# A matmul-with-rope kernel in pairs of tiles, with half of the transposes done by VectorE in 32x32 blocks and loaded in column quarters

## The chip, the cores and the metric

One core of one Trainium2 chip. The metric is the device time of one execution in microseconds (us), the median of several runs; fast runs of one kernel agree within 1.5%. The rounds ran on different chips (numbers 0, 5, 6 and 12 are on record), so each has its own runs of the kernel before. Some executions are told "slow" (over 1.5% above the fastest of the same kernel); ratios and readings below use fast runs, unless a sentence says otherwise.

TensorE is the matmul engine (PE in the profile; PEld is its weight load), VectorE is DVE, ScalarE is ACT, GpSimd is POOL and SyncE is SP. SP issues nearly all loads and ACT nearly all stores, on two queues that the profile calls q1 (SP) and q10 (ACT). The profile counts both against the same 16 DMA engines.

## The reference

Input x is 16 x 512 x 768 in fp32, the weight is 768 x 768, cos and sin are 512 x 64.

```python
y = np.matmul(x, weight).reshape(batch, seq, n_heads, head_dim)   # 12 heads of 64
y1, y2 = y[..., :32], y[..., 32:]
out1 = y1 * cos1 - y2 * sin1
out2 = y2 * cos2 + y1 * sin2
out = np.concatenate([out1, out2], axis=-1).reshape(batch, seq, hidden)
```

## The kernel before

The 8192 rows are cut in 64 tiles of 128 rows. A tile goes through: load (SP), cast to fp16 (ACT), six 128x128 transposes (PE, into PSUM), a copy back to SBUF (ACT), twelve matmuls (PE, six chunks of the 768 columns times two parts of the output), two multiplies by cos and sin (DVE), an add (POOL) and a store (ACT's queue). Row p of tile r of a batch is sequence row 4p + r, so each partition gets a whole row of 3072 B.

```python
xv = x.rearrange("b (p r) h -> b r p h", r=SB)          # SB = 4

def load(i):
    xss[i] = xpool.tile([P, H], FP32, tag="xs", name="xs")
    nc.sync.dma_start(out=xss[i], in_=xv[i // SB, i % SB])

wv = weight.rearrange("(kt p) n -> p kt n", p=P)

def load_w(kt):
    nc.sync.dma_start(out=w_raw[:, kt], in_=wv[:, kt])  # 128 rows of 3072 B

def transpose(i, eng):
    ...
    for kt in range(NKT):                               # NKT = 6
        nc.tensor.transpose(pt[:, kt, :], xc[:, ts(kt, P)], ident)
    xTT[i] = tpool.tile([P, NKT, P], FP16, tag="xT", name="xT")
    copy(eng, xTT[i], pt)

def rope(i, c0, n, ps, add_eng):
    ...
    nc.vector.tensor_tensor(out=tv..., in0=ps..., in1=cos_sb[:, sb, :]..., op=MULT)
    nc.vector.tensor_tensor(out=qv..., in0=ps...[:, :, ::-1, :], in1=tee_sb[:, sb, :]..., op=MULT)
    add_eng.tensor_tensor(out=ov[:, ds(c0, n)], in0=tv, in1=qv, op=ADD)
```

## Time and profile before

The median is 166.50 us (166.46 to 166.57, 4 runs). The profiled execution is another that took 168.71 us; its span, from the first to the last instruction of the program, is 166.9 us.

| what | before | read from |
|---|---|---|
| PE busy | 153.6 of 166.9 us, 92% | the page's busy times |
| per tile on PE | 1.95 us matmuls + 0.34 us transposes | the timeline |
| per tile on DVE | 0.96 + 0.95 us | the groups by form |
| per tile on ACT, POOL | 0.84 + 0.80 us, 1.82 us | the groups |
| DMA packets of 3072, 1536, 1024 B | median 121, 65, 46 ns | the packets of the trace |

First the page of the kernel before: PE's busy time, then two rows with the span in 40 slices (DMA: mean busy share of the 16 engines in tenths, 9 is 90% or more; and what they moved), the SP queue (packets, MB, share of 16 engines), and the chain of waits by engine.

```profile
PE 153.6 (92%) x1165; PEld 98.5 (59%) x1165; DVE 122.9 (74%) x142; ACT 97.9 (59%) x127; POOL 114.4 (69%) x67
...
DMA  4999999999999999999999999999999984345544
GB/s 128 405 402 403 403 404 369 301 375 406 340 372 343 328 350 345 350 326 381 335 327 370 347 330 351 337 327 361 368 349 350 300 323 170 146 161 192 213 166 188
...
q1 hardware_dynamic: 10368, 27.92, 49.5%
...
PE 88%; DMA 4%; ACT 2%; DVE 2%; issue 1%; SPq 1%; DVEq 0%
```

PE is the limit: 92% busy and 88% of the chain that ended last. The DMA row is at 9 nearly throughout, which looks like a second limit, but it isn't one. The queue's own waits of SP (what, in all us, how often, longest) show what its loads waited for:

```profile
SPq L75 <- ACT xc L69: 83.2, 47, 1.9
```

47 loads waited, 83.2 us in all, for a cast to set an input buffer free. Loads run as far ahead as the buffers allow. A DMA share near 1 at 350 GB/s is therefore no proof that DMA bounds anything.

The costliest groups of the page (line, engine, operation, names, shapes, count | busy us, mean ns | idle before, and what ended it):

```profile
L130 POOL TENSOR_TENSOR ov<-tv,qv 128x768 f32<-128x768 f32 x63 | 114.2, 1816 | 47.4 <-DVE qv L122 46.2
L103 PE MATMUL psy<-w_sb,xT 128*128 128x512 f16 x756 | 135.1, 329 | 2.5 <-ACT xT L69 1.8
...
L116 DVE TENSOR_TENSOR tv<-psy,cos_sb 128x768 f32<-128x768 f32 (+1 forms) x65 | 61.4, 944 | 31.7 <-PE psy L103 30.5
L69 ACT COPY xT<-pt 128x768 f16<-128x768 f16 x63 | 50.3, 798 | 51.2 <-PE pt L93 51.2
L122 DVE TENSOR_TENSOR qv<-psy,tee_sb 128x768 f32<-128x768 f32 (+1 forms) x65 | 60.7, 934 | 0.0
L69 ACT CAST xc<-xs 128x768 f16<-128x768 f32 x63 | 52.7, 836 | 5.8 <-DMA xs<-in_x_dram 5.8
L93 PE MATMUL pt<-ident,xc 128*128 128x128 f16 x384 | 31.9, 219 | 2.9 <-ACT xc L69 2.2
```

Every other engine has less than PE's 2.285 us to do per tile: the largest is DVE, two multiplies.

### The profile page before, as it was taken

Reading aid. Unit: us, or ns where it says so; the run is one execution under the profiler, and the core shown is the slowest. Engines: PE = TensorE matmul, PEld = TensorE weight load, DVE = VectorE, ACT = ScalarE, POOL = GpSimd, SP = SyncE. Lnnn points to the kernel's source line nnn. Section 1 sums busy time; section 2 is a strip of 40 time slices with the busy share of each in tenths; the row PEclk is TensorE's granted clock in tenths of the full one; section 3 lists DMA queues with packets and bytes.
Section 4 is the critical chain, followed back from the end, with each engine's and each line's share of the span. In section 5 each row is a group of like instructions: output and inputs, shape, how many; then the busy total and the mean of one; then the engine's idle time right before and its main releaser. Section 6 shows DMA issues by size and latency. Waiting matters only on the chain.

```text
span 166.9 us, 3136 instructions
## 1 busy us (share of the span) xinstructions
PE 153.6 (92%) x1165; PEld 98.5 (59%) x1165; DVE 122.9 (74%) x142; ACT 97.9 (59%) x127; POOL 114.4 (69%) x67
## 2 busy tenths in 40 slices
PE   7657699999999999999999999999999999999930
PEld 2224466666666666666666666666666666666610
DVE  0522598777877688877778877778877778777792
ACT  3053366667766667766667766667666667666400
POOL 0000099777787777887777887777887777877770
PEclk9987999999999999999999999999999999999997
DMA  4999999999999999999999999999999984345544
GB/s 128 405 402 403 403 404 369 301 375 406 340 372 343 328 350 345 350 326 381 335 327 370 347 330 351 337 327 361 368 349 350 300 323 170 146 161 192 213 166 188
DMA packets 19887, 53.19 MB, mean 319 GB/s; under 512 B 2336, under 2 KB 2848, under 8 KB 19872
## 3 DMA queue, kind: packets, MB, share of 16 engines
q1 hardware_dynamic: 10368, 27.92, 49.5%
q10 hardware_dynamic: 9504, 25.07, 37.8%
q8 instruction: 9, 0.15, 0.5%
q14 instruction: 6, 0.05, 0.1%
HBM read 27.82 MB, written 25.17 MB: 317 GB/s over the span
## 4 chain that ended last, share of the span: by engine, by line
PE 88%; DMA 4%; ACT 2%; DVE 2%; issue 1%; SPq 1%; DVEq 0%
PE psy L103 74%; PE pt L93 13%; DMA xs<-in_x_dram 4%; PE psy L216 1%; DVE ov L130 1%; ACT xc L69 1%; ACT xT L69 1%; DVE qv L122 1%; SPq L80 1%; DVE tv L116 0%; SPq L75 0%; DVEq L130 0%; DVEq L116 0%
## 5 line engine op out<-in xcount | busy, mean ns | idle before, releaser
L130 POOL TENSOR_TENSOR ov<-tv,qv 128x768 f32<-128x768 f32 x63 | 114.2, 1816 | 47.4 <-DVE qv L122 46.2
L103 PE MATMUL psy<-w_sb,xT 128*128 128x512 f16 x756 | 135.1, 329 | 2.5 <-ACT xT L69 1.8
L103 PEld LDWEIGHTS <-xT 128*128 128x128 f16 x756 | 71.8, 99 | 44.9 <-ACT xT L69 2.1
L116 DVE TENSOR_TENSOR tv<-psy,cos_sb 128x768 f32<-128x768 f32 (+1 forms) x65 | 61.4, 944 | 31.7 <-PE psy L103 30.5
L69 ACT COPY xT<-pt 128x768 f16<-128x768 f16 x63 | 50.3, 798 | 51.2 <-PE pt L93 51.2
L122 DVE TENSOR_TENSOR qv<-psy,tee_sb 128x768 f32<-128x768 f32 (+1 forms) x65 | 60.7, 934 | 0.0
L69 ACT CAST xc<-xs 128x768 f16<-128x768 f32 x63 | 52.7, 836 | 5.8 <-DMA xs<-in_x_dram 5.8
L93 PE MATMUL pt<-ident,xc 128*128 128x128 f16 x384 | 31.9, 219 | 2.9 <-ACT xc L69 2.2
L93 PEld LDWEIGHTS <-xc 128*128 128x128 f16 x384 | 26.6, 98 | 12.3 <-ACT xc L69 3.0
L83 DVE CAST w_sb<-w_raw 128x768 f16<-128x768 f32 x6 | 3.3, 558 | 4.1 <-DMA w_raw<-in_weight_dram 4.1
L141 PE MATMUL cold_ps<-cold 128*128 128x512 f16 x13 | 4.6, 514 | 1.2 <-DVE cold L146 1.2
L141 PEld LDWEIGHTS <-cold 128*128 128x128 f16 x13 | 1.5, 126 | 3.3 <-issue 1.9
L71 DVE CAST xc<-xs 128x768 f16<-128x768 f32 x1 | 0.6, 560 | 3.7 <-DMA xs<-in_x_dram 3.7
L69 ACT ACT_TABLE_LOAD x1 | 1.3, 1283 | 2.1 <-issue 2.1
L216 PE MATMUL psy<-w_sb,xT 128*128 128x384 f16 x12 | 2.1, 326 | 0.0
L130 DVE TENSOR_TENSOR ov<-tv,qv 128x384 f32<-128x384 f32 x2 | 1.7, 862 | 0.1
L216 PEld LDWEIGHTS <-xT 128*128 128x128 f16 x12 | 1.2, 98 | 0.8
L71 DVE COPY xT<-pt 128x768 f16<-128x768 f16 x1 | 0.6, 556 | 0.6 <-PE pt L93 0.6
L146 DVE MEMSET cold<- 128x256 uint32 x1 | 0.3, 272 | 0.9 <-PEq L244 0.9
L244 POOL MEMSET const-float32-0.0<- 128x1 f32 x1 | 0.1, 98 | 0.2 <-issue 0.2
L185 DVE TENSOR_SCALAR tee_sb<-tee_sb 128x128 f32<-128x128 f32 x1 | 0.2, 220 | 0.0
L244 POOL MEMSET const-bfloat16-1.0<- 128x1 bf16 x1 | 0.1, 101 | 0.0
(2 smaller groups left out, 0.2 us busy)
## 6 DMA issues: line engine op xcount, KB each, us to landing
xs<-in_x_dram SPq DMA_DIRECT2D x64, 384.0 KB, 5.6
out_dram<-ov ACTq DMA_DIRECT2D x63, 384.0 KB, 4.8
w_raw<-in_weight_dram SPq DMA_DIRECT2D x6, 384.0 KB, 5.9
out_dram<-ov SPq DMA_DIRECT2D x2, 192.0 KB, 2.2
cos_sb<-in_cos_dram ACTq DMA_DIRECT2D x1, 128.0 KB, 5.2
tee_sb<-in_sin_dram ACTq DMA_DIRECT2D x1, 128.0 KB, 6.2
ident<-identity ACTq DMA_DIRECT2D x1, 32.0 KB, 3.6
```

Source lines behind the costliest of these rows:

```text
L69: eng.copy(out=o, in_=i_)
L71: eng.tensor_copy(out=o, in_=i_)
L80: nc.sync.dma_start(out=w_raw[:, kt], in_=wv[:, kt])
L83: nc.vector.tensor_copy(out=w_sb[:, kt], in_=w_raw[:, kt])
L93: nc.tensor.transpose(pt[:, kt, :], xc[:, ts(kt, P)], ident)
L103: nc.tensor.matmul(psys[i][:, ds(noff, nsz)], xTT[i][:, kt, :], w_sb[:, kt, ds(noff % H, nsz)], start=(kt == 0), stop=(kt == NKT - 1),)
L116: nc.vector.tensor_tensor(out=tv.rearrange("p (h d) -> p h d", d=D), in0=ps.rearrange("p (h d) -> p h d", d=D), in1=cos_sb[:, sb, :].unsqu ...
L122: nc.vector.tensor_tensor(out=qv.rearrange("p (h t d) -> p h t d", t=2, d=HD), in0=ps.rearrange("p (h t d) -> p h t d", t=2, d=HD)[:, :, : ...
L130: add_eng.tensor_tensor(out=ov[:, ds(c0, n)], in0=tv, in1=qv, op=ADD)
L141: nc.tensor.matmul(cold_ps, cold[:, 0:P], cold, start=True, stop=True)
L146: nc.vector.memset(cold, 0.0)
L216: nc.tensor.matmul(psys[i][:, n, 0:sz], xTT[i][:, kt, :], w_sb[:, kt, ds(c0, sz)], start=(kt == 0), stop=(kt == NKT - 1),)
```

## The change

The intent is to give PE and DVE less to do.

1. Tiles are worked in pairs from two batches with the same rows, so the same cos and sin. One multiply of 3072 elements per partition (cos and sin products of both tiles) takes the place of four of 768.
2. The second tile of each pair isn't transposed by PE. DVE transposes it, and the kernel takes it that DVE's transpose works on 32x32 blocks, each by itself. So a block stays within its group of 32 partitions, and a group can hold only one quarter of the columns. The load has to put it there: group q of 32 partitions gets the column quarter q (192 columns, 768 B) of all 128 rows.
3. The weight rows have to follow the same order of columns: partition 32q + a of chunk (t, e) holds row 192q + 64t + 2a + e.

```diff
-    def load(i):
-        xss[i] = xpool.tile([P, H], FP32, tag="xs", name="xs")
-        nc.sync.dma_start(out=xss[i], in_=xv[i // SB, i % SB])
+    def load(n, s):
+        b, r = where(n, s)                      # 2 * (n // SB) + s, n % SB
+        ...
+        if by_blocks(n, s):                     # n > 1 and s == 1
+            xs = xs.rearrange("p (j k) -> p j k", j=NQ)
+            src = x[b].rearrange("(j a r) (q k) -> r j q a k", r=SB, a=R, q=NQ)
+            for j in range(NQ):
+                nc.sync.dma_start(out=xs[:, j], in_=src[r, j])
+        else:
+            nc.sync.dma_start(out=xs, in_=x[b].rearrange("(p r) h -> r p h", r=SB)[r])
-    wv = weight.rearrange("(kt p) n -> p kt n", p=P)
-        nc.sync.dma_start(out=w_raw[:, kt], in_=wv[:, kt])
+    wv = weight.rearrange("(q t a e) n -> t e q a n", q=NQ, t=NT, e=2)
+        nc.sync.dma_start(out=w_raw[:, t, e], in_=wv[t, e])
+    def transpose_blocks(n, s):
+        xT = tpool.tile([P, NT, P, 2], FP16, tag="xT", name="xT")
+        nc.vector.transpose(
+            out=xT.bitcast(FP32).rearrange("p t m e -> p (t m e)"),
+            in_=x16.pop((n, s)).bitcast(FP32).rearrange("p t j r -> p (t j r)"),
+        )
+        xTT[n, s] = xT.rearrange("p t m e -> p t e m")      # PE reads every second element
     def rope(...):
-        (two multiplies of 768)
+        nc.vector.tensor_tensor(                             # one of 3072
+            out=tq..., in0=psys[n]...broadcast_to((P, 2, nh, D)),
+            in1=csn[:, :, r, :]...broadcast_to((P, 2, nh, D)), op=MULT)
...
```

The change also has a longer prefetch (8 pairs instead of 8 tiles), other buffer counts and another order of start and end, which the cut above leaves out.

More of the change, by code (lines that the diff above doesn't have):

```diff
@@ L34, with where, by_blocks @@
     HD = D // 2
-    NKT = H // P
-    NMB = B * S // P
+    R = 32
+    NQ = P // R
+    KQ = H // NQ
+    NT = KQ // (2 * R)
     SB = S // P
-    NSPLIT = [(0, 512), (512, H - 512)]
-    HALVES = [(0, H // 2), (H // 2, H // 2)]
-    FIRST = 3
-    AHEAD = 8
-    xv = x.rearrange("b (p r) h -> b r p h", r=SB)
-    ov_dram = out.rearrange("b (p r) h -> b r p h", r=SB)
+    NP = B * SB // 2
+    CHUNKS = [(t, e) for t in range(NT) for e in range(2)]
+    DEPTH = 8
+    TAIL = 2
+    def where(n, s):
+        return 2 * (n // SB) + s, n % SB
+    def by_blocks(n, s):
+        return n > 1 and s == 1
     konst = ctx.enter_context(tc.tile_pool(name="konst", bufs=1))
     ident = konst.tile([P, P], FP16)
-    cos_sb = konst.tile([P, SB, D], FP32)
-    tee_sb = konst.tile([P, SB, D], FP32)
-    w_raw = konst.tile([P, NKT, H], FP32)
-    w_sb = konst.tile([P, NKT, H], FP16)
-    xpool = ctx.enter_context(tc.tile_pool(name="xpool", bufs=AHEAD + 3))
-    cpool = ctx.enter_context(tc.tile_pool(name="cpool", bufs=4))
-    tpool = ctx.enter_context(tc.tile_pool(name="tpool", bufs=FIRST + 2))
-    rpool = ctx.enter_context(tc.tile_pool(name="rpool", bufs=4))
-    opool = ctx.enter_context(tc.tile_pool(name="opool", bufs=5))
+    cold = konst.tile([P, 512], FP16)
+    sin_sb = konst.tile([P, SB, D], FP32)
+    csn = konst.tile([P, 2, SB, D], FP32)
+    w_raw = konst.tile([P, NT, 2, H], FP32)
+    w_sb = konst.tile([P, NT, 2, H], FP16)
+    xpool = ctx.enter_context(tc.tile_pool(name="xpool", bufs=2 * DEPTH + 2))
+    cpool = ctx.enter_context(tc.tile_pool(name="cpool", bufs=6))
+    tpool = ctx.enter_context(tc.tile_pool(name="tpool", bufs=7))
+    rpool = ctx.enter_context(tc.tile_pool(name="rpool", bufs=3))
+    opool = ctx.enter_context(tc.tile_pool(name="opool", bufs=4))
     pt_pool = ctx.enter_context(tc.tile_pool(name="pt", bufs=2, space=bass.MemoryType.PSUM))
-    py_pool = ctx.enter_context(tc.tile_pool(name="py", bufs=3, space=bass.MemoryType.PSUM))
-    cold = konst.tile([P, 512], FP16)
+    py_pool = ctx.enter_context(tc.tile_pool(name="py", bufs=2, space=bass.MemoryType.PSUM))
     cold_ps = pt_pool.tile([P, 512], FP32, tag="pt", name="cold_ps")
-    xss, x16, xTT, psys, ovs = {}, {}, {}, {}, {}
+    xss, x16, xTT, psys, tqs, ovs = {}, {}, {}, {}, {}, {}
     def copy(eng, o, i_):
@@ L71, in copy @@
             eng.tensor_copy(out=o, in_=i_)
-    def load(i):
-        xss[i] = xpool.tile([P, H], FP32, tag="xs", name="xs")
-        nc.sync.dma_start(out=xss[i], in_=xv[i // SB, i % SB])
-    wv = weight.rearrange("(kt p) n -> p kt n", p=P)
-    def load_w(kt):
-        nc.sync.dma_start(out=w_raw[:, kt], in_=wv[:, kt])
-    def cast_w(kt):
-        nc.vector.tensor_copy(out=w_sb[:, kt], in_=w_raw[:, kt])
-    def cast(i, eng):
-        x16[i] = cpool.tile([P, H], FP16, tag="xc", name="xc")
-        copy(eng, x16[i], xss.pop(i))
@@ L89, in transpose @@
-    def transpose(i, eng):
-        xc = x16.pop(i)
-        pt = pt_pool.tile([P, NKT, P], FP16, tag="pt", name="pt")
-        for kt in range(NKT):
-            nc.tensor.transpose(pt[:, kt, :], xc[:, ts(kt, P)], ident)
-        xTT[i] = tpool.tile([P, NKT, P], FP16, tag="xT", name="xT")
-        copy(eng, xTT[i], pt)
-    def mm(i, kt, parts=NSPLIT):
-        if i not in psys:
-            psys[i] = py_pool.tile([P, 2, 512], FP32, tag="psy", name="psy").rearrange(
+    def load(n, s):
+        b, r = where(n, s)
+        xs = xpool.tile([P, H], FP32, tag="xs", name="xs")
+        if by_blocks(n, s):
[4 more added lines that the diff above has]
+        else:
+            nc.sync.dma_start(
+                out=xs, in_=x[b].rearrange("(p r) h -> r p h", r=SB)[r]
+            )
+        xss[n, s] = xs
@@ new lines, with load_w, cast_w, cast @@
+    wv = weight.rearrange("(q t a e) n -> t e q a n", q=NQ, t=NT, e=2)
+    def load_w(t, e):
+        nc.sync.dma_start(out=w_raw[:, t, e], in_=wv[t, e])
+    def cast_w(t, e):
+        nc.vector.tensor_copy(out=w_sb[:, t, e], in_=w_raw[:, t, e])
+    def cast(n, s, eng):
+        xc = cpool.tile([P, H], FP16, tag="xc", name="xc")
+        x16[n, s] = xc.rearrange("p (t q r) -> p t q r", t=NT, q=NQ)
+        src = xss.pop((n, s))
+        if by_blocks(n, s):
+            src = src.rearrange("p j (t r) -> p t j r", t=NT)
+        else:
+            src = src.rearrange("p (q t r) -> p t q r", t=NT, q=NQ)
+        copy(eng, x16[n, s], src)
@@ new lines, in transpose @@
+    def transpose(n, s, eng):
+        xc = x16.pop((n, s)).rearrange("p t q (r e) -> p t e (q r)", e=2)
+        pt = pt_pool.tile([P, NT, 2, P], FP16, tag="pt", name="pt")
+        for t, e in CHUNKS:
+            nc.tensor.transpose(pt[:, t, e, :], xc[:, t, e, :], ident)
+        xT = tpool.tile([P, NT, 2, P], FP16, tag="xT", name="xT")
+        copy(eng, xT, pt)
+        xTT[n, s] = xT
+    def transpose_blocks(n, s):
[3 more added lines that the diff above has]
+            in_=x16.pop((n, s)).bitcast(FP32).rearrange("p t j r -> p (t j r)"),
+        )
+        xTT[n, s] = xT.rearrange("p t m e -> p t e m")
@@ L100, in mm @@
+    def mm(n, s, t, e, c0=0, c1=H):
+        if n not in psys:
+            psys[n] = py_pool.tile([P, 3, 512], FP32, tag="psy", name="psy").rearrange(
                 "p b n -> p (b n)"
             )
-        for noff, nsz in parts:
-            nc.tensor.matmul(
-                psys[i][:, ds(noff, nsz)],
-                xTT[i][:, kt, :],
-                w_sb[:, kt, ds(noff % H, nsz)],
-                start=(kt == 0),
-                stop=(kt == NKT - 1),
-            )
-    def rope(i, c0, n, ps, add_eng):
-        sb = i % SB
-        nh = n // D
-        tv = rpool.tile([P, H], FP32, tag="tv", name="tv")[:, :n]
-        qv = rpool.tile([P, H], FP32, tag="qv", name="qv")[:, :n]
+            if n < 2:
+                nc.tensor.matmul(
+                    psys[n][:, 512:1024], cold[:, 0:P], cold, start=True, stop=False
+                )
+        cut = 512 if s == 0 else 256
+        for lo, hi in ((0, cut), (cut, H)):
+            lo, hi = max(lo, c0), min(hi, c1)
+            joined = n < 2 and 512 <= s * H + lo < 1024
+            if lo < hi:
+                nc.tensor.matmul(
+                    psys[n][:, ds(s * H + lo, hi - lo)],
+                    xTT[n, s][:, t, e, :],
+                    w_sb[:, t, e, ds(lo, hi - lo)],
+                    start=((t, e) == CHUNKS[0] and not joined),
+                    stop=((t, e) == CHUNKS[-1] and not (joined and s == 0)),
+                )
@@ L116, in rope @@
+    def rope(n, c0, c1, add_eng):
+        r = n % SB
+        w = c1 - c0
+        nh = w // D
+        if n not in tqs:
+            tqs[n] = rpool.tile([P, 2, 2 * H], FP32, tag="tq", name="tq")
+            ovs[n] = opool.tile([P, 2 * H], FP32, tag="ov", name="ov")
+        tq = tqs[n][:, :, ds(c0, w)]
+        ov = ovs[n][:, ds(c0, w)]
         nc.vector.tensor_tensor(
-            out=tv.rearrange("p (h d) -> p h d", d=D),
-            in0=ps.rearrange("p (h d) -> p h d", d=D),
-            in1=cos_sb[:, sb, :].unsqueeze(1).broadcast_to((P, nh, D)),
+            out=tq.rearrange("p j (h d) -> p j h d", d=D),
+            in0=psys[n][:, ds(c0, w)].rearrange("p (h d) -> p h d", d=D)
+            .unsqueeze(1).broadcast_to((P, 2, nh, D)),
+            in1=csn[:, :, r, :].unsqueeze(2).broadcast_to((P, 2, nh, D)),
@@ L120, in rope @@
             op=MULT,
         )
-        nc.vector.tensor_tensor(
-            out=qv.rearrange("p (h t d) -> p h t d", t=2, d=HD),
-            in0=ps.rearrange("p (h t d) -> p h t d", t=2, d=HD)[:, :, ::-1, :],
-            in1=tee_sb[:, sb, :].rearrange("p (t d) -> p t d", t=2)
-            .unsqueeze(1).broadcast_to((P, nh, 2, HD)),
-            op=MULT,
-        )
-        ov = ovs[i]
-        add_eng.tensor_tensor(out=ov[:, ds(c0, n)], in0=tv, in1=qv, op=ADD)
-    def rope_whole(i):
-        ovs[i] = opool.tile([P, H], FP32, tag="ov", name="ov")
-        rope(i, 0, H, psys.pop(i)[:, 0:H], nc.gpsimd)
@@ L136, in store @@
-    def store(i):
-        nc.scalar.dma_start(out=ov_dram[i // SB, i % SB], in_=ovs.pop(i))
-    def warm(n):
-        for _ in range(n):
+        add_eng.tensor_tensor(
+            out=ov.rearrange("p (h t d) -> p h t d", t=2, d=HD),
+            in0=tq[:, 0].rearrange("p (h t d) -> p h t d", t=2, d=HD),
+            in1=tq[:, 1].rearrange("p (h t d) -> p h t d", t=2, d=HD)[:, :, ::-1, :],
+            op=ADD,
+        )
+    def store(n, eng, c0=0, c1=2 * H):
+        b, r = where(n, 0)
+        dst = out.rearrange("b (p r) h -> r p b h", r=SB)[r, :, b : b + 2]
+        src = ovs[n].rearrange("p (b h) -> p b h", b=2)
+        if c1 - c0 < 2 * H:
+            s = c0 // H
+            dst = dst[:, s, c0 - s * H : c1 - s * H]
+            src = src[:, s, c0 - s * H : c1 - s * H]
+        eng.dma_start(out=dst, in_=src)
@@ L141, in warm @@
+    def warm(k):
+        for _ in range(k):
             nc.tensor.matmul(cold_ps, cold[:, 0:P], cold, start=True, stop=True)
@@ L147 @@
     nc.scalar.dma_start(out=ident, in_=id_dram.ap())
-    load(0)
-    load_w(0)
-    load_w(1)
-    load(1)
-    nc.scalar.dma_start(out=cos_sb, in_=cos.rearrange("(p r) d -> p r d", r=SB))
-    nc.scalar.dma_start(out=tee_sb, in_=sin.rearrange("(p r) d -> p r d", r=SB))
-    load_w(2)
-    load_w(3)
-    load(2)
-    load_w(4)
-    load_w(5)
-    for i in range(FIRST, AHEAD):
-        load(i)
-    warm(9)
-    cast(0, nc.vector)
-    transpose(0, nc.vector)
-    warm(4)
-    for kt in (0, 1):
-        cast_w(kt)
-        mm(0, kt)
@@ L169 @@
-    cast(1, nc.scalar)
-    transpose(1, nc.scalar)
-    mm(1, 0)
-    mm(1, 1)
-    for kt in (2, 3):
-        cast_w(kt)
-        mm(0, kt)
-        mm(1, kt)
-    cast(2, nc.scalar)
-    transpose(2, nc.scalar)
-    for kt in range(4):
-        mm(2, kt)
-    cast_w(4)
-    for i in range(FIRST):
-        mm(i, 4)
-    cast_w(5)
+    for n in (0, 1):
+        for s in (0, 1):
+            load(n, s)
+    for t, e in CHUNKS:
+        load_w(t, e)
+    load(2, 0)
+    nc.sync.dma_start(out=csn[:, 0], in_=cos.rearrange("(p r) d -> p r d", r=SB))
@@ new lines @@
+    nc.sync.dma_start(out=sin_sb, in_=sin.rearrange("(p r) d -> p r d", r=SB))
+    load(2, 1)
+    for n in range(3, DEPTH):
+        for s in (0, 1):
+            load(n, s)
+    warm(8)
+    cast(0, 0, nc.vector)
+    transpose(0, 0, nc.vector)
+    cast(0, 1, nc.scalar)
+    warm(4)
+    transpose(0, 1, nc.scalar)
+    cast(1, 0, nc.vector)
+    warm(4)
+    transpose(1, 0, nc.vector)
+    cast(1, 1, nc.scalar)
+    warm(4)
+    transpose(1, 1, nc.scalar)
+    for k, c in enumerate(CHUNKS):
+        cast_w(*c)
+        mm(0, 0, *c)
+        mm(0, 1, *c)
+        if k == 0:
+            continue
+        mm(1, 0, *CHUNKS[k - 1])
@@ L185 @@
+    cast(2, 0, nc.scalar)
+    cast(2, 1, nc.scalar)
+    nc.vector.tensor_copy(out=csn[:, 1, :, 0:HD], in_=sin_sb[:, :, HD:D])
     nc.vector.tensor_scalar_mul(
-        out=tee_sb[:, :, 0:HD], in0=tee_sb[:, :, 0:HD], scalar1=-1.0
+        out=csn[:, 1, :, HD:D], in0=sin_sb[:, :, 0:HD], scalar1=-1.0
     )
-    cast(3, nc.scalar)
-    mm(0, 5)
-    rope_whole(0)
-    mm(1, 5)
-    rope_whole(1)
-    transpose(3, nc.scalar)
-    cast(4, nc.scalar)
-    mm(2, 5)
-    rope_whole(2)
-    for i in range(FIRST, NMB):
-        if i + AHEAD - FIRST < NMB:
-            load(i + AHEAD - FIRST)
-        if i + 1 < NMB:
-            transpose(i + 1, nc.scalar)
-        if 4 < i + 2 < NMB:
-            cast(i + 2, nc.scalar)
-        if i < NMB - 1:
-            for kt in range(NKT):
-                mm(i, kt)
-            rope_whole(i)
-            store(i - 3)
@@ L210 @@
-    i = NMB - 1
-    ovs[i] = opool.tile([P, H], FP32, tag="ov", name="ov")
-    for n, (c0, sz) in enumerate(HALVES):
-        for kt in range(NKT):
-            if i not in psys:
-                psys[i] = py_pool.tile([P, 2, 512], FP32, tag="psy", name="psy")
-            nc.tensor.matmul(
-                psys[i][:, n, 0:sz],
-                xTT[i][:, kt, :],
-                w_sb[:, kt, ds(c0, sz)],
-                start=(kt == 0),
-                stop=(kt == NKT - 1),
-            )
-    for j in range(NMB - 4, NMB - 1):
-        store(j)
@@ L225 @@
-    for n, (c0, sz) in enumerate(HALVES):
-        rope(i, c0, sz, psys[i][:, n, 0:sz], nc.vector)
-        nc.sync.dma_start(out=ov_dram[i // SB, i % SB, :, ds(c0, sz)], in_=ovs[i][:, ds(c0, sz)])
+    rope(0, 0, 2 * H, nc.gpsimd)
+    mm(1, 0, *CHUNKS[-1])
+    transpose(2, 0, nc.scalar)
+    for c in CHUNKS:
+        mm(1, 1, *c)
+    transpose_blocks(2, 1)
+    cast(3, 0, nc.scalar)
+    cast(3, 1, nc.scalar)
+    rope(1, 0, 2 * H, nc.gpsimd)
+    transpose_blocks(3, 1)
+    for n in range(2, NP):
+        if n + DEPTH - 2 < NP:
+            for s in (0, 1):
+                load(n + DEPTH - 2, s)
+        if n < NP - 1:
+            for c in CHUNKS:
+                mm(n, 0, *c)
+            if n + 1 < NP:
+                transpose(n + 1, 0, nc.scalar)
+            for c in CHUNKS:
+                mm(n, 1, *c)
+            if n + 2 < NP:
+                cast(n + 2, 0, nc.scalar)
+                cast(n + 2, 1, nc.scalar)
+            if n >= 3:
+                store(n - 3, nc.scalar)
+            if n < NP - TAIL:
+                rope(n, 0, 2 * H, nc.gpsimd)
+            else:
+                rope(n, 0, H, nc.gpsimd)
+                rope(n, H, 2 * H, nc.gpsimd)
+            if n + 2 < NP:
+                transpose_blocks(n + 2, 1)
@@ L231 @@
+    n = NP - 1
+    for c in CHUNKS:
+        mm(n, 0, *c)
+    for c in CHUNKS:
+        mm(n, 1, *c, 0, H // 3)
+    for c in CHUNKS:
+        mm(n, 1, *c, H // 3, H)
+    store(n - 3, nc.scalar)
+    store(n - 2, nc.scalar)
+    store(n - 1, nc.sync)
+    rope(n, 0, H, nc.gpsimd)
+    store(n, nc.scalar, 0, H)
+    m = H + H // 3
+    rope(n, H, m, nc.gpsimd)
+    rope(n, m, 2 * H, nc.vector)
+    store(n, nc.sync, H, m)
+    store(n, nc.scalar, m, 2 * H)
 _INS = ['x', 'weight', 'cos', 'sin', 'n_heads']
```

## The prediction

> **What bounds it now.** TensorE: on the page PE is busy 92% of 166.9 us, and the chain of waits is 88% PE. From 21 us to 160 us it repeats, per 128-row tile, 1.95 us of matmuls plus 0.34 us for six transposes: 2.285 us x 61 = 139 us; the tail is 6 us. The groups give, per tile, VectorE 0.96 + 0.95 us, ScalarE 0.84 + 0.80, GpSimd 1.82, all below that. Most DMA packets of 3072 B take 121 ns, of 1536 B about 65, of 1024 B 46: about 8 ns + 0.037 ns per byte on one DMA engine. Loads run about 11 tiles ahead; nothing in the steady state waits for them.
>
> **Engines after the change, per pair of tiles (estimates from those durations).** PE: 2 x 1.95 + 0.34 = 4.24 us instead of 4.57. VectorE: one 3072-element multiply, from 957 ns at 768 and 550 at 384 about 3.4 us instead of 3.8, plus a transpose of about 0.55: 3.95. GpSimd about 3.6, ScalarE 2.5. Two pairs fit in PSUM, so it stays PE-bound: 30 x 4.24 plus a shorter start would give about 151 us, if loads kept up. Strided weight loads (step 2) should cost nothing visible.
>
> **What decides it: the loads.** The quarter loads and all six weight loads now walk DRAM as 4 column quarters x 32 rows, the 4 outermost; the tile side is 128 partitions. [...] Before, transfers had 128 outermost: 16 engines[...]. After, it gives 4[...]. Their work, estimated with the packet times above:
> - weights 6 x 32 x 121 ns = 23 us (6 us over 16 engines);
> - quarter loads 30 tiles x 4 x 32 packets of 768 B at about 37 ns = 141 us;
> - whole loads 34 x 8 x 121 ns = 33 us, stores 64 x 8 x 121 ns = 62 us.
> Together 259 us that the other twelve engines can't relieve; per pair 4.7 + 0.97 + 1.94 = 7.6 us against 4.24 of PE. So the span becomes DMA-bound: 2 us to the first packet, 259, less the last five pairs' stores (10), plus about 11 after the last load: about 264 us, with rounding and latency.
>
> **Predicted: 264 us, 230 to 288. Faster by over 2%: 0.20; within 2%: 0.02; slower by over 2%: 0.78.** The faster share is the case that transfers spread over 16 engines after all (about 151 us).
>
> **What would show it.** The DMA row's mean busy share falls from 0.98 to 0.4 to 0.6, GB/s to about 200. A weight load takes about 4 us by itself; the last weight chunk's matmuls start near 31 us instead of 14. Casts on ScalarE wait for loads in every pair; the chain of waits is mostly DMA; PE busy falls near 60%, and its granted clock may drop in the gaps. Multiply 3.4 us, block transpose 0.55, GpSimd add 3.6 test the engine costs.
>
> **What would make it wrong.** A spread over 16 engines (then 151 us, unless the GpSimd add with reversed halves takes over 4.24 us and bounds it); 768 B packets far from 37 ns; four engines running faster while twelve idle.

The sum: 23 + 141 + 33 + 62 = 259 us, and 2 + 259 - 10 + 11 = 262, "about 264" with rounding and latency. But the four engines that the first two terms are divided by, and that all four terms fall on the same ones, were the estimate when this was written. The trace of the kernel after shows the four (1112 end packets, below); that they are the same ones is inferred there. Two pairs do fit in PSUM: the kernel after ran with two such buffers.

## The result

The kernel after takes 268.92 us (median of 267.36 to 270.26, 4 fast runs), beside 166.50 us before: ratio 1.6147, 95% interval 1.6055 to 1.624, slower. A ratio is the mean time of one kernel's fast runs over that of the other's fast runs of the same rounds, so it isn't quite the ratio of the medians quoted. The predicted 264 us is 1.8% below the median.

The page of the kernel after, the same rows and the granted TensorE clock (in tenths) besides:

```profile
PE 168.5 (63%) x994; PEld 95.0 (36%) x994; DVE 131.6 (49%) x79; ACT 73.3 (27%) x95; POOL 110.0 (41%) x38
...
PEclk9955569998898997997557797989996599999995
DMA  6225255466665657564546646666554678646386
GB/s 237 104 103 161 100 150 166 136 232 227 229 216 197 220 175 246 187 228 149 165 136 231 224 163 209 227 218 211 202 199 138 228 264 332 257 163 236 146 328 236
...
q1 hardware_dynamic: 22232, 28.71, 32.8%
...
SPq 39%; DMA 35%; POOL 10%; issue 8%; ACT 2%; PE 2%; DVE 1%; POOLq 0%; ACTq 0%; DVEq 0%
```

PE fell from 92% to 63% busy and DMA from about 320 to 199 GB/s in the mean, with a share of 0.5 to 0.6. In the second and third slice (7 to 20 us), when the weights are loaded, the share is 2 tenths and the rate 103 to 104 GB/s: a quarter of the 402 to 405 GB/s that the kernel before reached in its second to sixth slice. SyncE's queue heads the chain, at 39%. I read that as back-pressure and not as a longer instruction: issuing a whole-tile load, a plain transfer like the one before, took SP 1.56 us in the median instead of 0.33.

Two of the waits (who waited for what: us in all, times, longest us) of the kernel after:

```profile
ACT xT L76 <- DMA xs<-in_x_dram: 71.8, 9, 21.9
...
ACT xc L76 <- DMA xs<-in_x_dram: 52.7, 13, 21.3
```

ScalarE waits for loads, singly up to 22 us. (The first line is no cast: the copy xT needs no load, but stands behind a store in ACT's order, which waits for a load to land; see cols4 below.) In the kernel before, the casts' wait for loads came to 5.8 us, all at the start. The longest piece of the chain, in order of time (start us, us, what), is the weights:

```profile
8.55 23.09 DMA w_raw<-in_weight_dram
```

And the group of the weight casts (engine, operation, times of one, first and last start), with what it waited for:

```profile
L100 DVE CAST w_sb<-w_raw x6: 559/560/561, 11.6 to 31.7; 128x768 f16<-128x768 f32 x6
...
  DMA w_raw<-in_weight_dram: 19.0, 6
```

Six casts from 11.6 to 31.7 us, on average 4.0 us apart. Last, the engine costs, from the groups by form:

```profile
L169 POOL TENSOR_TENSOR ov<-tq 128x1536 f32<-128x1536 f32 x30 | 103.4, 3449 | 152.7 <-DMA out_dram<-ov 107.1 <-DVE tq L162 45.6
L162 DVE TENSOR_TENSOR tq<-psy,csn 128x3072 f32<-128x3072 f32 x30 | 100.5, 3351 | 43.2 <-PE psy L145 43.1
L145 PEld LDWEIGHTS <-xT 128*128 128x128 f16 x768 | 78.0, 105 | 150.7 <-ACT xT L76 83.5 <-issue 28.3
...
L123 DVE STREAM_TRANSPOSE xT<-xc 128x384 f32<-128x384 f32 x30 | 17.2, 575 | 60.0 <-ACT xc L76 60.0
```

The packets of the trace tell how many engines took part, by their number. Before, the SP queue had 72 transfers and 1152 packets of 4 bytes, 16 for each. I read them as one end packet from each engine that works on a transfer. After:

| SP transfers of the kernel after | count | engines if all 16 | engines if quarters and weights use 4 |
|---|---|---|---|
| whole tiles of x | 34 | 544 | 544 |
| column quarters | 120 | 1920 | 480 |
| weights | 6 | 96 | 24 |
| cos, sin, last stores | 4 | 64 | 64 |
| sum (measured: 1112) | 164 | 2624 | 1112 |

The count is 1112 exactly: quarter loads and weights, with four entries in the slowest dimension in DRAM, ran on four engines. Which four they are, the packets don't tell; that they are always the same four is inferred from the rate of 103 to 104 GB/s above, with several weight loads in flight: from 9 to 20 us four packets are under way in 88% of the moments (sampled every 10 ns), five or six in the rest, never fewer. The time follows from the packet times, summed: quarter packets 567 us over 4 engines = 142 us, weights 768 packets at about 0.13 us over 4 = 25 us, the other loads about 43 us over 16, and the stores 62 us over 16. That is 272 us of packet time on each of the four engines, more than the span of 266.7 us: packets of one engine then overlap in time (the share of all 16, a sum of packet times too, came to 1.03 from 8 to 25 us in the kernel before), so the sum tells that the four were full, and isn't itself a time. (The third term is the rest of the loads' packet time after the weights.) In every stretch that I summed between 10 and 220 us (20 to 40 us each), it comes to 1.10 to 1.16 of the stretch. The other twelve engines have 105 us of packet time.

The loads don't bind to the end, though. The last packet of 768 B ends at 234.1 us, and from 217 us on PE runs without a stop, a pair every 4.24 us. The last issue of quarter loads and the last matmuls of the timeline:

```profile
215.15 8.09 SPq L87 DMA_DIRECT2D xs<-in_x_dram  x4
...
251.62 6.01 PE L145 MATMUL psy<-w_sb,xT 128*128 128x256 f16 x36
```

### The profile page after: what moved, and what is told of

Its sections match the earlier page's. It is cut to its first block, busy times and chain, and to the rows that moved or that the text cites. A ratio compares the mean times of both kernels' runs of the same rounds, so it can differ in the third digit from the quotient of the medians.

```text
span 266.7 us, 2682 instructions
## 1 busy us (share of the span) xinstructions
PE 168.5 (63%) x994; PEld 95.0 (36%) x994; DVE 131.6 (49%) x79; ACT 73.3 (27%) x95; POOL 110.0 (41%) x38
## 4 chain that ended last, share of the span: by engine, by line
SPq 39%; DMA 35%; POOL 10%; issue 8%; ACT 2%; PE 2%; DVE 1%; POOLq 0%; ACTq 0%; DVEq 0%
SPq L87 26%; DMA xs<-in_x_dram 18%; SPq L89 11%; POOL ov L169 10%; DMA w_raw<-in_weight_dram 9%; DMA out_dram<-ov 8%; PE psy L145 2%; SPq L97 2%; ACT xc L76 2%; DVE tq L162 1%; ACT xT L76 1%; POOLq L315 0%; ACTq L184 0%; PE pt L116 0%; ACTq L76 0%
## 5 line engine op out<-in xcount | busy, mean ns | idle before, releaser
L145 PE MATMUL psy<-w_sb,xT 128*128 128x512 f16 (+1 forms) x768 | 153.0, 356 | 87.5 <-ACT xT L76 75.4
L169 POOL TENSOR_TENSOR ov<-tq 128x1536 f32<-128x1536 f32 (+2 forms) x34 | 109.8, 3237 | 152.7 <-DMA out_dram<-ov 107.1
L145 PEld LDWEIGHTS <-xT 128*128 128x128 f16 x768 | 78.0, 105 | 150.7 <-ACT xT L76 83.5
L162 DVE TENSOR_TENSOR tq<-psy,csn 128x3072 f32<-128x3072 f32 (+3 forms) x35 | 107.4, 3077 | 44.0 <-PE psy L145 43.9
L76 ACT CAST xc<-xs 128x768 f16<-128x768 f32 x62 | 50.0, 834 | 56.0 <-DMA xs<-in_x_dram 52.7
L76 ACT COPY xT<-pt 128x768 f16<-128x768 f16 x32 | 25.5, 798 | 122.2 <-DMA xs<-in_x_dram 71.8
L123 DVE STREAM_TRANSPOSE xT<-xc 128x384 f32<-128x384 f32 x30 | 17.2, 575 | 60.0 <-ACT xc L76 60.0
L116 PE MATMUL pt<-ident,xc 128*128 128x128 f16 x204 | 18.8, 234 | 0.4 <-DVE xc L78 0.4
L116 PEld LDWEIGHTS <-xc 128*128 128x128 f16 x204 | 15.9, 107 | 7.5 <-issue 2.2
L188 PE MATMUL cold_ps<-cold 128*128 128x512 f16 x20 | 7.4, 520 | 1.2 <-DVE cold L193 1.2
```

The source lines that it names most:

```text
L76: eng.copy(out=o, in_=i_)
L116: nc.tensor.transpose(pt[:, t, e, :], xc[:, t, e, :], ident)
L123: nc.vector.transpose(out=xT.bitcast(FP32).rearrange("p t m e -> p (t m e)"), in_=x16.pop((n, s)).bitcast(FP32).rearrange("p t j r -> p (t ...
L145: nc.tensor.matmul(psys[n][:, ds(s * H + lo, hi - lo)], xTT[n, s][:, t, e, :], w_sb[:, t, e, ds(lo, hi - lo)], start=((t, e) == CHUNKS[0] ...
L162: nc.vector.tensor_tensor(out=tq.rearrange("p j (h d) -> p j h d", d=D), in0=psys[n][:, ds(c0, w)].rearrange("p (h d) -> p h d", d=D) .uns ...
L169: add_eng.tensor_tensor(out=ov.rearrange("p (h t d) -> p h t d", t=2, d=HD), in0=tq[:, 0].rearrange("p (h t d) -> p h t d", t=2, d=HD), in ...
```

## The experiments

The theory was: the four engines are the whole cause, and engine costs are as predicted, so that 151 us are left when all transfers use 16. Rivals: the small 768 B packets; the number of transfers; the slower PE weight loads or the paired DVE and POOL instructions. The first four runs tested it, the others followed what was left. In all tables "ratio" is against the kernel before in the same rounds.

### q16: the quarter loads alone, meant for 16 engines

The four transfers of a tile are cut by column quarter instead of by 32 rows. They have the same 512 packets of 768 B, to the same places.

```diff
-            src = x[b].rearrange("(j a r) (q k) -> r j q a k", r=SB, a=R, q=NQ)
-            for j in range(NQ):
-                nc.sync.dma_start(out=xs[:, j], in_=src[r, j])
+            src = x[b].rearrange("(j a r) (q k) -> r q a j k", r=SB, a=R, q=NQ)
+            for q in range(NQ):
+                nc.sync.dma_start(out=xs[q * R : (q + 1) * R], in_=src[r, q])
```

> The changed kernel, with each block tile still loaded by four transfers of 128 packets of 768 B, but each transfer now fills one group of 32 partitions, so that 32 is the slowest dimension on both sides. Weights as in the change. Four-engine theory: 16 engines each, 4.7 us per tile falls to 1.2; the weights still take until about 31 us, then PE-bound at 4.24 us a pair: 34.5 + 30 x 4.24 + 9 = about 171 us. Rival 'small packets or too many transfers' (same packets, same number of transfers): stays near 267 us. Rival 'GpSimd, VectorE or strided weight loads are slower than costed': stays over 200 us.

Measured: 192.86 us (192.38 and 193.34), ratio 1.1523 (1.1408 to 1.1639), correct. 76 us of the loss are gone with the order of two dimensions, at the same packets and the same number of transfers. Small packets and the count can't be the main cause. The DMA share from 80 to 160 us is 0.99 to 1.00, at 321 to 324 GB/s; in the kernel after it was 0.54 to 0.60, at 178 to 209 GB/s. But the expectation was 22 us too low.

### w16: the weights alone, meant for 16 engines

```diff
-        nc.sync.dma_start(out=w_raw[:, t, e], in_=wv[t, e])
+        for q in range(NQ):
+            nc.sync.dma_start(out=w_raw[q * R : (q + 1) * R, t, e], in_=wv[t, e, q])
```

> The changed kernel with only the six weight loads each split in four transfers of 32 partitions[...], the quarter loads untouched. Four-engine theory: 23 us of weights on four engines become 6, everything else stays: about 269 - 17 = 252 us. Rival 'the weights are not the matter or more transfers cost': 265 us or more.

Measured: 257.52 us (257.45 and 257.58), ratio 1.5386 (1.5239 to 1.5534), correct. The weights account for 11 us; 17 were expected. (The 6 us in the expectation suppose 16 engines for each weight transfer. The engines of this run weren't counted; in qw16, with the same weight loads, the last weight cast starts at 18.2 us instead of 31.7.)

### qw16: both

> Both edits together. Four-engine theory: what the pairs were meant to give, PE-bound at 4.24 us a pair and about 151 us, faster than the kernel before by 9%; mean DMA share over 0.9 in the steady state. If issuing 24 weight transfers at about 0.4 us each paces the start, 2 us more. Rival 'small packets': over 200 us.

Measured: 180.75 us (180.13 to 183.88, 4 runs, one of them slow), ratio of fast runs 1.077 (1.0667 to 1.0874), correct. So the spread over four engines accounts for 88 of the 102 us that the change cost (net: each transfer now also fills 32 partitions and not 128, which helps nothing, as shown below). But this is 30 us above the 151 us that the prediction named for a spread over 16, and slower than before. Something else is in the way. The rows of its page:

```profile
DMA  5977899998999999898989999899999999986996
GB/s 177 310 207 211 253 253 221 216 366 279 289 334 296 360 263 388 220 359 288 317 295 250 402 241 385 251 359 306 304 365 247 379 289 353 259 310 239 392 395 240
```

And ACT's wait for loads:

```profile
ACT xc L76 <- DMA xs<-in_x_dram: 69.6, 41, 9.2
```

Loads arrive just as they are needed and DMA moves 306 GB/s from 40 to 100 us, though its engines look full (share 0.97). A pair takes 4.9 us (40 to 150 us), against PE's 4.24. The 768 B packets took 45.9 ns in the mean (36 in the median) instead of 36.9 in the kernel after.

### b4 and b16: four and sixteen entries in the kernel before

The kernel before, nothing changed but the order of rows in its loads: 4 x 32 or 16 x 8 (wrong, rows are permuted). The packets stay whole rows of 3072 B.

```diff
-        nc.sync.dma_start(out=xss[i], in_=xv[i // SB, i % SB])
+        nc.sync.dma_start(out=xss[i],        # q = 4 for b4, 16 for b16
+            in_=x[i // SB].rearrange("(a q r) h -> r q a h", r=SB, q=4)[i % SB])
```

> The kernel before, with only its x loads' source rows taken in a permuted order, so that 4 x 32 rows can't be merged and the slowest dimension in DRAM is 4: one transfer a tile, packets of 3072 B, same bytes, nothing else changed; its numbers are wrong on purpose. Four-engine theory: 64 x 32 x 121 ns = 248 us of loads on four engines + 62 us stores + 6 us weights, about 320 us; DMA share about 0.4. Rival 'small packets, more transfers or the compute side': stays at 166.5 us.

> The control for b4: the kernel before with the x rows permuted in the same way, but as 16 x 8 rows, so that the slowest dimension is 16 (wrong numbers on purpose). Four-engine theory: 16 engines, 166.5 us as before. If the permuted order of rows in DRAM or the three-dimensional pattern made b4 slow, it stays far over 200.

Measured: b4 328.61 us (328.43 and 328.80), ratio 1.9634; b16 174.07 us (173.85 and 174.30), ratio 1.0375 (1.024 to 1.051). With four entries outermost the tuned kernel takes twice its time, at the same packets, bytes and number of transfers; with 16 it is 3.8% slower. So the number of entries of the slowest dimension makes the difference. The end packets agree: the SP queue has 384 in b4 (64 x 4 + 8 x 16) and 1152 in b16 (72 x 16). The 3.8% of b16 weren't expected. The trace tells where they arise, but not why: from 10 to 30 us its DMA moved 288 and 269 GB/s per 10 us at a full share, the kernel before 401 and 378; from 60 to 100 us the rates are alike (354 and 346). The pages of b4 and, below it, b16:

```profile
DMA  7722332334265634334443443444344432225454
GB/s 166 196 100 101 141 140 103 140 139 176 107 248 219 242 133 176 160 158 177 176 163 154 177 177 140 177 176 162 154 179 176 166 150 106 104 116 235 196 226 172
...
DMA  4999999999999999999999999999999994444444
GB/s 108 332 301 306 241 241 308 326 321 367 392 414 410 399 398 350 356 346 352 335 353 355 338 361 324 360 331 344 359 332 340 331 355 178 183 183 184 188 183 183
```

In b4 the share goes mostly to 3 or 4 tenths, and the rate mostly to 140 to 180 GB/s.

### whole: what the engines cost when loads are plain

The kernel with both loads regrouped, but a block tile is loaded by one plain transfer of 128 rows (wrong; every engine does the same work).

```diff
-            src = x[b].rearrange("(j a r) (q k) -> r q a j k", r=SB, a=R, q=NQ)
-            for q in range(NQ):
-                nc.sync.dma_start(out=xs[q * R : (q + 1) * R], in_=src[r, q])
+            nc.sync.dma_start(out=xs..., in_=x[b].rearrange("(p r) h -> r p h", r=SB)[r])
```

> qw16 with each block tile loaded by one plain transfer of 128 packets of 3072 B (wrong numbers on purpose: the block transpose needs the quarters). All compute instructions stay. If the engine costs are as predicted (multiply 3.36, block transpose 0.57, GpSimd add 3.45, measured), it is PE-bound at 4.24 us a pair: 155 us with the start of qw16, which is 4 us late. If something in compute (step-2 weight loads, the GpSimd add) also limits qw16, it stays over 170.

Measured: 163.0 us (162.37 and 163.63), ratio 0.9715 (0.9564 to 0.9867), two runs; by the 2% rule of the record this is unclear, and it is 8 us over the 155 expected. So with plain loads the change would bring some 3%, give or take 1.5. Its timeline (start us, us, engine, line, operation, count; idle before) in the steady state:

```profile
100.18 4.06 PE L147 MATMUL psy<-w_sb,xT 128*128 128x256 f16 x24
...
101.44 0.57 DVE L125 STREAM_TRANSPOSE xT<-xc 128x384 f32<-128x384 f32 x1
101.61 3.47 POOL L171 TENSOR_TENSOR ov<-tq 128x1536 f32<-128x1536 f32 x1 [0.38 <-DVE tq L164]
...
102.40 3.36 DVE L164 TENSOR_TENSOR tq<-psy,csn 128x3072 f32<-128x3072 f32 x1 [0.39 <-PE psy L147]
...
104.42 4.06 PE L147 MATMUL psy<-w_sb,xT 128*128 128x256 f16 x24
```

Two groups of 24 matmuls start 4.24 us apart, and DVE needs 3.36 + 0.57 us and POOL 3.46 us for a pair. PE bounds the pair, as predicted, and its weight loads from every second element cost nothing that shows (4.24 us is what the times of the kernel before gave for a pair). DMA moves 414 GB/s from 40 to 100 us here.

### cols4 and pad1: number of transfers, or small packets?

cols4 keeps four transfers per block tile, but each is one column quarter of all 128 rows to all 128 partitions. pad1 brings the tile in one transfer of 512 packets of 768 B, to all 128 partitions (a padded buffer keeps the four pieces of a row apart). Their outputs are wrong, which doesn't matter for the times.

```diff
+            # cols4
+            src = x[b].rearrange("(p r) (q k) -> r q p k", r=SB, q=NQ)
+            for q in range(NQ):
+                nc.sync.dma_start(out=xs[:, q], in_=src[r, q])
+            # pad1: xp is [P, H + 64], xs its view without the padding
+            nc.sync.dma_start(out=xs,
+                in_=x[b].rearrange("(p r) (q k) -> r p q k", r=SB, q=NQ)[r])
```

> qw16 with the same four transfers of 128 packets of 768 B per block tile, but each over all 128 partitions (128 rows x one column quarter; wrong numbers on purpose). Theory 'groups of 32 partitions slow the packets' (46 ns in qw16 against 37): about 155 to 160 us, packets back at 37 ns. Theory 'too many transfers: eight semaphores in rotation, so that loads wait for stores': stays near 181. Theory 'small packets': stays near 181.

> qw16 with one transfer per block tile that still moves 512 packets of 768 B over 128 partitions (its four quarters land 200 elements or so apart; wrong numbers on purpose). Theory 'too many transfers': about 155 us. Theory 'groups of 32 partitions': about 155 us as well. Theory 'small packets': near 181. Together with the other two: a high cols4 and a low pad1 mean the number of transfers, both high the packet size, both low the groups of 32.

Measured: cols4 183.92 us (183.30 and 184.55), ratio 1.0962 (1.0798 to 1.1127). pad1 168.14 us (166.37 in a fast run; its profiled run of 169.91 counts as slow, so no ratio is given); 155 was expected. Size of packet isn't it: pad1 has the same 15360 packets of 768 B at 36.8 ns and moves 394 GB/s from 40 to 100 us. I took this for proof of the number of transfers, which the next experiment upset.

### batch and batch12: few transfers, into one group of 32 partitions

Here a correct kernel gets by with one transfer of 512 packets per block tile, on average. If partition 32q + a holds rows 16a to 16a + 15 of a batch, a transfer brings column quarter q of four tiles at once, and DVE writes its transpose with a stride so that rows come in the right order. A pair then needs three transfers instead of six. Pairs 0 to 3 use PE's transposes.

```diff
+    def load_batch(g, q):
+        if g not in xbs:
+            xbs[g] = bpool.tile([P, P // R * SB, KQ], FP32, tag="xb", name="xb")
+        nc.sync.dma_start(
+            out=xbs[g][q * R : (q + 1) * R],
+            in_=x[2 * g + 1].rearrange("(a i) (q k) -> q a i k", a=R, q=NQ)[q])
...
-            out=xT.bitcast(FP32).rearrange("p t m e -> p (t m e)"),
+            out=xT.bitcast(FP32).rearrange("p t (a j) e -> p t j (a e)", a=R),
```

batch12 also loads the weights in 12 transfers of 6144 B packets.

> Correct kernel. The kernel with both loads regrouped, but one transfer of 512 packets of 768 B brings one 32-partition group of four tiles at once (rows in the order that a 32-partition group wants, VectorE writes the transpose with a stride), so a pair needs 3 transfers instead of 6; pairs 0 to 3 use PE transposes. Packets are as small as before and each transfer still fills one 32-partition group. Number-of-transfers theory: PE-bound, 4.24 us per pair, 163 to 168 us, ScalarE no longer waiting for loads after the start. If small packets into one 32-partition group are the limit: packets near 46 ns and about 180 us. If the strided transpose write takes over 0.9 us instead of 0.57, VectorE bounds the pair at over 4.3 us.

> The same, with the weights in 12 transfers of 6144 B packets instead of 24 of 3072 B. The issue of a load takes about 0.4 us on SyncE, so the last weight chunk is there some 3 to 4 us earlier: 2 to 4 us less than the same kernel with 24 weight transfers, so 160 to 165 us if that one is PE-bound, and then faster than the kernel before.

Measured: batch 183.57 us (181.55 to 185.85, two of four runs slow), ratio of fast runs 1.0816 (1.0726 to 1.0906); batch12 181.89 us (180.00 to 187.75, two slow), ratio 1.0733 (1.0642 to 1.0823). Both are correct, and not faster than with six transfers. The page of batch12 (a fast run):

```profile
DMA  5999999999999999999999999999999995845867
GB/s 175 319 233 233 367 213 246 352 229 396 383 252 216 363 404 328 211 242 409 406 264 220 357 410 345 226 286 407 399 231 217 384 413 201 339 191 194 339 262 271
```

And its transpose from the groups by form:

```profile
L130 DVE STREAM_TRANSPOSE xT<-xc 128x384 f32<-128x384 f32 x28 | 24.7, 882 | 12.3 <-ACT xc L77 12.3
```

The strided transpose takes 882 instead of 575 ns, which brings DVE to 3.36 + 0.88 = 4.24 us, level with PE; that alone can't make 180 us. The DMA row is full at 200 to 400 GB/s, and packets are slow: 768 B took 54.0 ns in the mean, against 36.8 in pad1 with as many transfers. So halving the number of transfers bought nothing where each transfer fills one group of 32 partitions.

Put side by side, all with small packets but whole:

(The times are medians of all runs. Of fast runs alone, batch12 has 180.00 and 180.37, pad1 166.37; pad1's packets and rate are from its slow run.)

| kernel | transfers per pair | a block transfer fills | mean 768 B packet | 40 to 100 us | time |
|---|---|---|---|---|---|
| qw16 | 6 | 32 partitions | 45.9 ns | 306 GB/s | 180.75 us |
| batch12 | 3 | 32 partitions | 54.0 ns | 315 GB/s | 181.89 us |
| cols4 | 6 | 128 partitions | 39.0 ns | 326 GB/s | 183.92 us |
| pad1 | 3 | 128 partitions | 36.8 ns | 394 GB/s | 168.14 us |
| whole | 3 | 128 partitions | (3072 B: 121 ns) | 414 GB/s | 163.0 us |

Only few transfers that also spread over all partitions are fast. I read this as two obstacles, of which taking away either one alone brings nothing. It is a reading of five kernels and not a clean test: batch12 differs from pad1 also in the order of its loads and in the slower transpose.

For the first, 32 partitions, the weight loads can be looked at alone. The weights' stretch of qw16 (207 and 211 GB/s in its third and fourth slice, 9 to 18 us) doesn't show it: SP there issues one transfer of 96 KB every 0.46 us, which allows no more than 214 GB/s, and the DMA share is 0.75. batch12, with 192 KB in each transfer, shows it better. From 9 to 15 us it loads only weights and moves 237 GB/s at a share of 1.03 (the kernel before 404), SP issues only every 0.8 us though an issue takes 0.31, and the packets of 6144 B take 421 ns, where two of 3072 B take 242 in the kernel before. Why transfers into 32 partitions are slow isn't shown.

For the second, the number of transfers, there is a trace reading but no test. In these kernels all transfers share eight semaphores in rotation (the traces show eight numbers), and a transfer is only issued when the one before it on its semaphore, be it load or store, has landed: so it is for all 207 in cols4 that have one before them. With six transfers per pair that is little more than a pair earlier, and a store on ACT's queue can wait for a load that was issued only just before and is meant for a pair far ahead. The timeline of ACT in cols4:

```profile
82.66 1.57 ACT L76 CAST xc<-xs 128x768 f16<-128x768 f32 x2
89.06 0.38 ACTq L185 DMA_DIRECT2D out_dram<-ov  x1
89.54 0.80 ACT L76 COPY xT<-pt 128x768 f16<-128x768 f16 x1 [5.31 <-DMA xs<-in_x_dram]
```

ACT ends its casts at 84.2 us, issues the store only at 89.1, and makes the next copy, for which PE waits, after that: 5.31 us idle, ended by a load. The load on the store's semaphore had been issued at 84.35 us and landed at 88.99. ACT's waits of this kind, before a copy, came to 20.0 us (for loads) and 18.9 us (for stores) in that run. From 30 us on PE stops ten times for more than 0.3 us, 17.4 us in all, and every time ACT had held a store back until the transfer before it on its semaphore landed. pad1 has one such stop (3.2 us). In qw16 PE stops eight times (11.5 us), never behind such a store; there the casts wait for their loads. So the trace of cols4 shows the tie at work, but no run took away the tie alone.

### qw16_d5: a shorter prefetch distance

```diff
-    DEPTH = 8
+    DEPTH = 5
```

> The kernel with both loads regrouped (180.75 us), with only the prefetch distance cut from 8 pairs to 5. Theory 1, casts and stores are tied to far prefetch loads through the transfers' shared, rotating semaphores: a shorter distance loosens the tie, 165 to 170 us. Theory 2, six transfers per pair with a few in flight can't be put through faster, whatever the order: unchanged, 178 to 184 us. In the trace of the kernel with both loads regrouped, loads arrive just as they are needed, so theory 2 is the likelier.

Measured: 179.74 us (178.90 to 182.25, one of four slow), ratio of fast runs 1.0672 (1.0581 to 1.0762). No change beyond the spread, as the second theory had it. But in the trace of qw16 no store was held back by its semaphore, so there was no such tie to loosen, and this doesn't test what holds cols4 up. That test is missing.

### mix: meant to be the fastest

Two repairs. A different order of columns over the chunks (partition p holds weight rows 6p to 6p + 5) makes the weights six plain transfers again. And only every third pair has a block tile, so 40 small transfers are left of 120.

```diff
-        return n > 1 and s == 1
+        return n > 1 and n % EVERY == 2 and s == 1     # EVERY = 3
...
-    wv = weight.rearrange("(q t a e) n -> t e q a n", q=NQ, t=NT, e=2)
+    wv = weight.rearrange("(p t e) n -> t e p n", t=NT, e=2)
...
+        copy(eng, xc.rearrange("p (t m e) -> p t m e", t=NT, e=2),
+             src.rearrange("p (m t e) -> p t m e", t=NT, e=2))
...
+                if not by_blocks(n + 1, 1):
+                    transpose(n + 1, 1, nc.scalar)
```

> Correct kernel, meant to be the fastest. Against the kernel with both loads regrouped: (1) the order of the 768 columns over chunks is chosen so that a partition's six weight rows are neighbours in DRAM; the weights then are 6 plain transfers of 128 rows again, and the casts read pairs of columns with a stride; (2) only every third pair has its second tile transposed by VectorE (10 tiles, 40 small transfers instead of 120), the others by TensorE. TensorE: 20 x 4.575 + 10 x 4.235 = 134 us for 30 pairs instead of 139 us for 61 tiles before, minus the start, whose last weights should be there near 13 us instead of 18. If the loads keep up: 160 to 165 us. If the strided casts take over 1.1 us instead of 0.83, ScalarE comes near the pair's time and this shows as waits for xc. If small transfers still hold the loads back: 168 to 172 us.

Measured: 168.07 us (166.77 to 169.87, 6 runs, one slow), ratio of fast runs 1.0009 (0.9944 to 1.0074), correct: the same as before, and not the 160 to 165 expected. It is the best correct version of the change, and it doesn't beat the kernel before. The weights are repaired: the rate at the start is back, as the page shows in its first slices (343, 411 and 318 GB/s in the second to fourth).

```profile
GB/s 166 343 411 318 350 258 326 345 356 323 364 389 412 370 397 404 348 387 370 349 345 329 415 364 351 378 348 397 412 396 199 190 190 154 190 151 152 371 250 256
```

PE has 2.4 us less to do than before (151.2 instead of 153.6 us). Part of it went in two stops of PE, near 78 and 98 us (3.1 us in all, none in the kernel before), both behind a store that ACT held back as in cols4. The rest is seen at the end of the two timelines. Before, the last matmuls and the last instruction of any engine:

```profile
158.00 2.11 PE L216 MATMUL psy<-w_sb,xT 128*128 128x384 f16 x12
...
163.41 0.56 DVE L130 TENSOR_TENSOR ov<-tv,qv 128x384 f32<-128x384 f32 x1
```

In mix:

```profile
151.43 6.01 PE L148 MATMUL psy<-w_sb,xT 128*128 128x256 f16 x36
...
152.51 9.88 POOL L172 TENSOR_TENSOR ov<-tq 128x1536 f32<-128x1536 f32 x5 [1.11 <-DVE tq L165]
...
161.07 0.75 DVE L172 TENSOR_TENSOR ov<-tq 128x512 f32<-128x512 f32 x1
```

PE ends at 160.1 us before and at 157.4 us in mix, 2.7 us earlier. But after it come 6.8 us before (span 166.9) and 8.5 us in mix (165.9): POOL has a queue of large adds to finish when PE is done. The pairs give 1.7 us back in the tail. What is left of the gain, 1.0 us between these two profiled runs (168.71 and 167.68 us), is within the spread.

### What couldn't be tried

The plain way out would be one transfer with rows slowest and column quarters inside, meant to fill all partitions at once. No run of it is on record, so this stays open.

## Why the prediction was right

- "TensorE" bounds the kernel before: right. PE was busy 92%, and loads waited for buffers (83.2 us), not PE for loads.
- Four engines for quarter loads and weights: right, by the count of 1112 end packets, the 2-tenths share at 103 GB/s, by q16 and w16, and by b4, where the pattern alone doubled the time of the kernel before.
- "768 B at about 37 ns": 36.9 ns measured, 142 us over four engines (141 predicted). Weights "about 4 us each": casts 4.0 us apart, the last at 31.7 us, and the last chunk's matmuls at 32.3 us (31 predicted).
- The sum "259 us" and the total: here luck helped. The sum takes packet times to follow one another, but they overlap: up to 234.1 us, when the last load landed, the four engines had 259 us of packet time each. The prediction's terms put that moment at about 251 us (2 + 259 - 10), 17 us too late. After it came not "about 11" but 32.6 us, because some five pairs were still to be multiplied at 4.24 us each before the tail of 9 us. The two misses cancel: the four engines are shown, the closeness of 264 (1.8% low) isn't its merit alone.
- Share 0.4 to 0.6, about 200 GB/s, PE near 60%: 0.57, 199, 63%. The granted clock fell to 0.846 in the mean, from 0.983. In the page's rows it drops in and just after PE's gaps (0.5 where PE is at 0, at 127 to 140 us), so I take it for a consequence of waiting; no run tested it.
- "Casts on ScalarE wait for loads in every pair": the wait is there (52.7 us), but in 13 long waits and not in every pair. "The chain of waits is mostly DMA": in part. DMA has 35%, and SP's queue, which I read as held up by the same engines, 39%.
- Engine costs: multiply 3.35 us (3.4), transpose 0.575 (0.55), POOL 3.45 (3.6), a pair on PE 4.24 us (4.24, shown by whole).
- The step that failed is a branch that didn't come about: "would give about 151 us, if loads kept up". Loads regrouped for 16 engines (share 0.97 in qw16) took 180.75 us, and even plain loads 163.0 us. Two terms were wrong. "If loads kept up" was taken for granted for 16 engines; 32-partition transfers and six transfers per pair each prevent it. And 24 us for start and end together (151 less 30 x 4.24) was too small: in whole it was 161.8 - 127 = 35 us, of which 9.0 us came after the last matmul, and PE stopped once more near 58 us (1.4 us).

Of the loss of 102 us, 88 us are shown to come from the four engines (qw16 against after). The rest, 14 us, and the 3.5 us gain that was missed, come from the loads too: whole, with plain loads and all else as in qw16, takes 17.75 us less than qw16. How these split between the 32 partitions and the number of transfers isn't settled. (whole and qw16 ran in different rounds; against the kernel before in their own, the ratios are 0.9715 and 1.077.)

## What to carry to other kernels

Before changing a layout, look at the slowest dimension of each load in DRAM: four entries there put a transfer on four of 16 DMA engines here (1112 end packets where 16 engines would give 2624), and the same kernel took 328.61 us with four entries and 174.07 us with 16 (b4, b16). A low DMA share (0.57) together with waits for loads (52.7 us of casts), and end packets that are too few, shows it in a profile. After that, ask which partitions one transfer fills and how many transfers a step needs; here only loads over all 128 partitions in few transfers (394 and 414 GB/s in pad1 and whole, 306 to 326 in the others of the table) kept up with an engine that needed 371 GB/s (four tiles of 393 KB in 4.24 us). Small packets cost something too: by the median times of the kernel after, 768 B in 36 ns are 21 B per ns, and 3072 B in 121 ns are 25. And when a saving of a few per cent comes from larger instructions, look at the end of the kernel, where the last large instructions stand alone (8.5 us after PE's end in mix, 6.8 us before).
